# Moving the branches of an expert's second token block in a sparse expert loop

## The chip, the cores and the metric

One core of a Trainium2 chip runs the whole program as one launch. The metric is device time in microseconds (us): the median of 3 executions is 1828.38 us (1827.23 to 1830.39). Every trace number comes from one further execution that was profiled; it took 1832.22 us, of which the trace's span covers 1830.4 us.

Engines: PE is TensorE (PEld its weight loads), DVE is VectorE, ACT is ScalarE, POOL is GpSimd, and SP issues the large DMAs. Each works through its own instructions in the order in which they were written, and semaphores let one engine wait for another.

## The reference, cut to what matters

The program is one layer over 1024 tokens of 1024 channels: a token mixer and then a mixture of 32 experts, of which each token uses two. The change lies in the experts alone. The reference computes them so:

```python
def _expert_block(args):
    xblk, e = args                       # 128 token rows of one expert
    hid = jax.nn.silu(xblk @ w_gate[e]) * (xblk @ w_up[e])
    return hid @ w_down[e]
# block_e: an expert with n assigned tokens has ceil(n / 128) blocks
yb = lax.map(_expert_block, (xb, block_e))
out = jnp.einsum('tkd,tk->td', y.astype(f32), weights)
```

Gate and up weights are 1024 x 512, the down weight is 512 x 1024, all fp32. How many blocks an expert has is known only when the program runs.

## The kernel before, in words

The experts run one after another in a Python loop that is unrolled (`for e in range(NE)`, L1862). Each fp32 matrix is split into a high part (`hi`, a copy by ACT with rounding, L92) and a low part (`lo`, raw minus hi, by DVE, L93), and a product is summed from hi·hi, hi·lo and lo·hi (`mm3`, L96 to L98). An expert's weights are six loads of 1 MB (numbers 0 to 3 are gate and up, 4 and 5 down). `spl(e, i)` splits load `i` of expert `e` in two halves: two copies by ACT and two subtractions by DVE, and then SP issues a further load into the buffer that came free. The split halves go into ten buffers that are used in turn, so a new split waits until TensorE has done with what lay in its buffer.

For each expert the loop does:

- `xhalf` (L1686): four transposes of half of the 128 gathered tokens by PE into a `tp` buffer (there are two), then a split of the result by ACT and DVE. `XA` is the first half of the channels, `XB` the second.
- `part(e, q, os, ...)`: gate (`o` 0) and up (`o` 1) products over one half of the channels into two PSUM banks. An expert with at most 64 tokens takes a form with two products where others have three (L1697).
- `copies` (L1710): ACT copies the two sums out of PSUM (`sg`, `su`); DVE makes a small matrix `sm` (L1707).
- `fold` (L1719 to L1721): PE transposes both copies against `sm` into the two `tp` buffers, ACT takes silu, DVE multiplies, and the result is split into `hh` and `hl`.
- `down` (L96 to L98, `y<-...`): the down product, 24 matmuls, into the `y` banks.
- `emit`: DVE weighs the two banks into `yt` (L1736), POOL scatters them to memory (L1743).

While expert `e` is finished, the gate and up products of `e+1` are already begun: `part(e+1, 0, ...)` stands on both sides of `fold`. The two pairs of gate and up banks, `A` and `B`, change roles from expert to expert.

An expert with more than 128 tokens has a second block. It is done in `tc.If` blocks on a count that each engine loads into a register: `over(e, q, banks)` is transposes, split and products of the second block, `cso` are its copies (`og`, `ou`), and a fold, a down product and an `emit` of its own follow. The engines don't meet at such a block. An engine that skips it still adds, at its end, what the block's instructions would have added to its semaphore (an event at the line of the `If`). So an instruction behind the block that shares a tile with it waits until the other engine's sequencer has passed the block. With the inputs of this run 5 of the 32 experts have a second block (10 `yt` operations out of a `tp` buffer, two each).

In the kernel before, four such blocks stand in a round: L1871 (second half of `over` and `cso`), L1882 (the gather of a later second block), L1887 (fold of the second block) and L1893 (its down product at L1894, and at L1899 the first half of `over` of the next expert).

Of the kernel before, what the change touches and what calls it, by code (L numbers as in the profile page):

```python
# [20 lines left out]
P = 128  # L21
# [29 lines left out]
def block_kernel(ctx: ExitStack, tc: tile.TileContext, I, out):  # L51
# [3 lines left out]
    def pool(stack, name, bufs=1, **kw):  # L55
        return stack.enter_context(tc.tile_pool(name=name, bufs=bufs, reuse_waits="tile", **kw))
# [8 lines left out]
    def sb(pl, name, shape, dtype=F32, **kw):  # L65
        return pl.tile(shape, dtype, tag=kw.pop("tag", name), name=name, **kw)
# [24 lines left out]
    def split(hi, lo, src, eng=None):  # L91
        S.activation(hi, src, AF.Copy)  # L92
        (eng or V).tensor_tensor(lo, src, hi.bitcast(F32), op=ALU.subtract)  # L93

    def mm3(ps, a, b, first, last):
        PE.matmul(ps, a[0], b[0], start=first, stop=False)  # L96
        PE.matmul(ps, a[0], b[1], start=False, stop=False)  # L97
        PE.matmul(ps, a[1], b[0], start=False, stop=last)  # L98

    def warm(ps, us):  # L100
        for _ in range(round(us / 0.425)):
            PE.matmul(ps[:, 0:256], ident, ident.unsqueeze(1).to_broadcast([P, 2, P]), start=True, stop=True)
# [1079 lines left out]
    def granule(x, dtype=F32R):  # L1182
        a, b = (hip if x < NK - 3 else hia, lop) if x < NK else (hi2, lo2)
        return sb(a, "hi", [P, D], dtype), sb(b, "lo", [P, D], dtype)
# [337 lines left out]
    def dma_w():  # L1522
        x = next(ahead, None)
        if x is not None:
            RAW[x] = sb(bigp, "raw", [P, 2 * D])
            ld(RAW[x], I["w_exp"][seq[x[0]], x[1]])
        elif len(XL) < 5:
            t_ = sb(bigp, "raw", [P, 2, D])
            if len(XL) < 4:
                ld(t_, x1_d[2 * len(XL):2 * len(XL) + 2].rearrange("t p d -> p t d"))  # L1530
            else:
                ld(t_[:, 0], I["ln2_g"].partition_broadcast(P))
                ld(t_[:, 1], I["ln2_b"].partition_broadcast(P))
            XL.append(t_)
# [15 lines left out]
    def gather(xg, e, b):  # L1550
        if e < NE:
            G.indirect_dma_start(out=xg, out_offset=None, in_=h2_d,  # L1552
                                 in_offset=bass.IndirectOffsetOnAxis(ap=tbi[:, b, seq[e], 0:1], axis=0),
                                 bounds_check=T - 1, oob_is_err=False)
# [99 lines left out]
    psm = pool(mo, "psm", space=PSUM)  # L1654
# [6 lines left out]
    def spl(e, i, parts=(0, 1), refill=True):  # L1661
        if e >= NE:
            return
        for n in parts:
            a, b = granule(next(gi) % (NK + 2))
            split(a, b, RAW[e, i][:, n * D:(n + 1) * D], G if (i, n) in POOL_LO else V)
            SP[e, i, n] = (a, b)
        if 1 in parts:
            del RAW[e, i]
            if refill:  # L1670
                dma_w()

    def piece(e, i, k, n):
        z, w = n * k // D, n * k % D
        return tuple(t_[:, w:w + n] for t_ in SP[e, i, z])
# [6 lines left out]
    def xhalf(xg, q, nm="x"):  # L1682
        xs = sb(wk, f"{nm}{q if nm == 'x' else 0}", [P, 4, P, 2], F32R)
        pt = sb(psm, "tp", [P, 4, P], bufs=2)
        for z in range(4):
            PE.transpose(pt[:, z, :], xg[:, (4 * q + z) * P:(4 * q + z + 1) * P], ident)  # L1686
        split(xs[:, :, :, 0], xs[:, :, :, 1], pt)
        return xs
# [16 lines left out]
    def copies(e, pgu, nm="s", blk=0):  # L1705
        fm = sb(wk, nm + "m", [P, P])
        V.scalar_tensor_tensor(fm, both, few[:, blk, seq[e]:seq[e] + 1], ident, op0=ALU.mult, op1=ALU.add)  # L1707
        cs = [sb(wk, nm + x, [P, FF]) for x in "gu"]
        for c, ps_ in zip(cs, pgu):
            S.activation(c, ps_, AF.Copy)  # L1710
        return cs, fm

    def fold(cs, a="hh", b="hl"):
        (g, u), fm = cs
        a, b = sb(wk, a, [P, 4, P], F32R), sb(wk, b, [P, 4, P], F32R)
        pts = [sb(psm, "tp", [P, 4, P], bufs=2) for _ in range(2)]
        for src, pt in ((g, pts[0]), (u, pts[1])):
            for k in range(4):
                PE.matmul(pt[:, k, :], src[:, k * P:(k + 1) * P], fm, start=True, stop=True)  # L1719
        S.activation(g, pts[0].rearrange("p a b -> p (a b)"), AF.Silu)  # L1720
        V.tensor_mul(g, g, pts[1].rearrange("p a b -> p (a b)"))  # L1721
        split(a, b, g.rearrange("p (a b) -> p a b", a=4))
        return a, b

    def down(e, hs, py):
        for k in range(4):
            w = piece(e, 4 + k // 2, k % 2, D)
            for n in range(2):
                c = slice(n * 512, (n + 1) * 512)
                mm3(py[n], (hs[0][:, k, :], hs[1][:, k, :]), (w[0][:, c], w[1][:, c]), k == 0, k == 3)  # L1730

    def weigh(py, e, b):
        yt = sb(wk, "yt", [P, D])
        for n in range(2):
            c = slice(n * 512, (n + 1) * 512)
            V.scalar_tensor_tensor(yt[:, c], py[n], tbf[:, b, seq[e], 2:3], g2[:, c], op0=ALU.mult, op1=ALU.mult)  # L1736
        return yt

    def emit(py, e, b):
        scatter(weigh(py, e, b), e, b)  # L1740

    def scatter(yt, e, b):
        G.indirect_dma_start(out=y_d, out_offset=bass.IndirectOffsetOnAxis(ap=tbi[:, b, seq[e], 1:2], axis=0),  # L1743
                             in_=yt, in_offset=None, bounds_check=2 * T - 1, oob_is_err=False)

    def over(e, q, banks):
        if q == 0:
            warm(banks[0], 1.3)
        xs = xhalf(xos[e % 2], q, "o")
        part(e, q, range(2), xs, banks, 1)  # L1750
# [37 lines left out]
    def get_nb(e):  # L1788
        if e not in NBV:
            NBV[e] = load_nb(e)  # L1790
        return NBV[e]
# [14 lines left out]
    ybank = [sb(psm, f"y{n}", [P, 512]) for n in range(2)]  # L1806
# [55 lines left out]
    for e in range(NE):  # L1862
        nxt = e + 1 < NE
        A, B = GU[e % 2], GU[(e + 1) % 2]
        if nxt:
            XA = xhalf(xgs[(e + 1) % NX], 0)
            few_nb(e + 1)
        part(e, 1, range(2), XB, A)
        cs = copies(e, A)
        spl(e + 1, 1)  # L1870
        with tc.If(get_nb(e) > 1):  # L1871
            over(e, 1, B)
            cso = copies(e, B, "o", 1)
        if not nxt:
            spl(e, 4)
            spl(e, 5)
        if nxt:
            spl(e, 4)
            part(e + 1, 0, (0,), XA, B)
        hs = fold(cs)  # L1880
        if e + 2 < NE:
            with tc.If(get_nb(e + 2) > 1):  # L1882
                gather(xos[e % 2], e + 2, 1)
        if nxt:
            spl(e, 5)
            part(e + 1, 0, (1,), XA, B)
        with tc.If(get_nb(e) > 1):  # L1887
            h_ = fold(cso, "oh", "ol")
        if nxt:
            XB = xhalf(xgs[(e + 1) % NX], 1)  # L1890
            gather(xgs[(e + 1) % NX], e + 1 + NX, 0)
            down(e, hs, ybank)
        with tc.If((load_pair(e) if nxt else get_nb(e)) > 1):  # L1893
            with tc.If(get_nb(e) > 1):  # L1894
                banks = [sb(psm, "tp", [P, 512], bufs=2) for _ in range(2)]
                down(e, h_, banks)
                emit(banks, e, 1)
            if nxt:
                with tc.If(get_nb(e + 1) > 1):  # L1899
                    over(e + 1, 0, A)  # L1900
        if not nxt:
            down(e, hs, ybank)
            wf = sum([list(granule(next(gi) % (NK + 2), F32)) for _ in range(6)], [])
            with tc.If(load_nb(nbm) > 2):
                overflow(wf)
            for _ in range(3):
                y_raw()
            YT += [wf[2 * i:2 * i + 2] for i in range(5)]
            for i in range(NT):
                y_load(i)  # L1910
            tk = sb(wk, "tk", [P, NT])
            V.scalar_tensor_tensor(tk, iota[:, 0:NT], -float(P), tbf[:, 0, seq[e], 0:1].to_broadcast([P, NT]), op0=ALU.mult, op1=ALU.add)
            oh = xgs[2]
            for i in range(NT):
                V.tensor_scalar(oh[:, i * P:(i + 1) * P], iota[:, 0:P], tk[:, i:i + 1], None, op0=ALU.is_equal)
        spl(e + 1, 2)
        spl(e + 1, 3)
        if nxt:
            emit(ybank, e, 0)
        spl(e + 2, 0)  # L1920
# [9 lines left out]
    banks = [GU[0], GU[1], [sb(psm, "tp", [P, 512], bufs=2) for _ in range(2)], ybank]  # L1930
# [125 lines left out]
```

## Time and profile before

| | |
|---|---|
| median of 3 runs | 1828.38 us |
| the profiled execution | 1832.22 us, span 1830.4 us |
| PE busy | 1593.2 us, 87% of the span |
| DVE busy | 1338.5 us, 73% |
| ACT busy | 769.1 us, 42% |
| POOL busy | 308.4 us, 17% |
| loop over the experts | from about 905 us to 1755 us in the span |

An engine's busy share is an average over stages. The loop's stretch has to be read by itself: which engine waits in it, for whom, and what ends the wait. In the rows below "ACTq L1871" names an engine's sequencer at a line: the wait ended when ACT had passed the block at L1871.

### The profile page before, as it was taken

To read this page: it belongs to the slowest core of one execution; us is meant where nothing else is said; L and a number is where in the kernel's file an instruction comes from. 1 tells how busy PE (TensorE), PEld (TensorE's weight loads), DVE (VectorE), ACT (ScalarE), POOL (GpSimd) and SP (SyncE) were. 2 spreads that over 40 slices of the span, in tenths; PEclk is the share of its full clock that TensorE was granted. 3 is DMA by queue.
4 is the path that set the end of the run, shared out by engine and by line. 5 is a ranking of instruction groups with operands and counts; after the bars stand their busy time and mean duration, and the time that the engine had idled before them with its cause. 6 is when DMAs were issued, how large, how long until landed. Compare 5 with 4: busy or idle time off the path is not lost. (4 is left out here: it accounts for less than half of the span.)

```text
span 1830.4 us, 24156 instructions
## 1 busy us (share of the span) xinstructions
PE 1593.2 (87%) x7662; PEld 1256.8 (69%) x7662; DVE 1338.5 (73%) x2961; ACT 769.1 (42%) x1126; POOL 308.4 (17%) x264
## 2 busy tenths in 40 slices
PE   7999999999988999998877878777787888879775
PEld 3788887788877877887666656666566666767652
DVE  7768854699975787877757567777657777475768
ACT  2433323421133422212156455666556666464532
POOL 1530000022242000221211011011111111020117
PEclk9999999999999999998999998999999899999987
DMA  8327788523257564643448567788748778575663
GB/s 319 134 72 231 213 255 266 190 98 101 74 138 173 179 197 154 242 184 119 146 152 300 198 241 271 288 287 302 265 152 317 260 291 299 186 266 184 230 253 122
DMA packets 141759, 382.05 MB, mean 209 GB/s; under 512 B 17632, under 2 KB 76160, under 8 KB 116992
## 3 DMA queue, kind: packets, MB, share of 16 engines
q1 hardware_dynamic: 130912, 362.80, 57.4%
q0 software_dynamic: 10656, 16.80, 2.5%
q8 instruction: 108, 1.77, 0.4%
q14 instruction: 83, 0.68, 0.1%
HBM read 336.98 MB, written 68.76 MB: 222 GB/s over the span
## 5 line engine op out<-in xcount | busy, mean ns | idle before, releaser
L93 DVE TENSOR_TENSOR lo<-raw,hi 128x1024 fp32r<-128x1024 f32 x376 | 442.8, 1221 | 147.2 <-ACT hi L92 138.8
L92 ACT ACTIVATE hi<-raw 128x1024 fp32r<-128x1024 f32 x376 | 373.4, 1049 | 119.3 <-PEq L1893 39.8
L96 PE MATMUL g<-hh,wh 128*128 128x512 f32 x448 | 176.9, 395 | 0.0
L98 PE MATMUL g<-hh,wl 128*128 128x512 f32 x448 | 174.7, 390 | 0.0
L97 PE MATMUL g<-hl,wh 128*128 128x512 f32 x448 | 174.6, 390 | 0.0
L1743 POOL DMA_INDIRECT y_d<-yt,tbi x37 | 65.9, 1780 | 399.0 <-DVE yt L1736 300.3
L1697 PE MATMUL g<-hi,x 128*128 128x512 f32 x168 | 76.9, 458 | 54.4 <-DVE x L93 37.7
L96 PE MATMUL y<-hi,hh 128*128 128x512 f32 x256 | 108.1, 422 | 5.1 <-ACTq L1887 5.1
L1552 POOL DMA_INDIRECT xg<-h_d,tbi x32 | 40.4, 1264 | 381.8 <-PE tp L1686 314.7
L98 PE MATMUL y<-hi,hl 128*128 128x512 f32 x256 | 104.6, 409 | 0.0
L97 PE MATMUL y<-lo,hh 128*128 128x512 f32 x256 | 104.3, 407 | 0.0
L96 PEld LDWEIGHTS g<-hh,wh 128*128 128x128 f32 x448 | 84.1, 188 | 19.1 <-issue 2.3
L98 PEld LDWEIGHTS g<-hh,wl 128*128 128x128 f32 x448 | 84.1, 188 | 18.0
L93 POOL TENSOR_TENSOR wl<-raw,wh 128x1024 fp32r<-128x1024 f32 x17 | 41.0, 2409 | 329.4 <-ACT wh L92 329.4
L97 PEld LDWEIGHTS g<-hl,wh 128*128 128x128 f32 x448 | 84.1, 188 | 16.7
L1686 PE MATMUL tp<-ident,xg 128*128 128x128 f32 x256 | 41.3, 285 | 54.5 <-ACTq L1887 40.1
L1697 PEld LDWEIGHTS g<-hi,x 128*128 128x128 f32 x168 | 35.0, 208 | 71.8 <-ACTq L1871 60.9
L1686 PEld LDWEIGHTS tp<-ident,xg 128*128 128x128 f32 x256 | 27.4, 141 | 77.8 <-ACTq L1887 51.2
L611 ACT ACTIVATE sg<-g 128x512 f32<-128x512 f32 x32 | 19.2, 599 | 140.1 <-PE g L98 104.8
L1697 PE MATMUL g<-lo,x 128*128 128x512 f32 x168 | 74.1, 441 | 1.6 <-DVE lo L93 1.6
L912 DVE TENSOR_TENSOR vs<-vs,sa 128x32 f32<-128x32 f32 x512 | 75.2, 201 | 0.0
L1697 PE MATMUL u<-hi,x 128*128 128x512 f32 x168 | 67.7, 403 | 0.0
(537 smaller groups left out, 3868.3 us busy)
## 6 DMA issues: line engine op xcount, KB each, us to landing
raw<-in_w_exp SPq DMA_DIRECT2D x192, 1024.0 KB
raw<-in_w_r SPq DMA_DIRECT2D x28, 512.0 KB
w<-w_d SPq DMA_DIRECT2D x32, 384.0 KB
raw<-in_w_ada SPq DMA_DIRECT2D x20, 512.0 KB
sig_d<-sg SPq DMA_DIRECT2D x32, 256.0 KB
rp<-r_d SPq DMA_DIRECT2D x64, 128.0 KB
raw<-in_w_ada SPq DMA_DIRECT2D x6, 1024.0 KB
aw<-in_w_ada SPq DMA_DIRECT2D x12, 512.0 KB
```

What stands on the lines that cost most here:

```text
L92: S.activation(hi, src, AF.Copy)
L93: (eng or V).tensor_tensor(lo, src, hi.bitcast(F32), op=ALU.subtract)
L96: PE.matmul(ps, a[0], b[0], start=first, stop=False)
L97: PE.matmul(ps, a[0], b[1], start=False, stop=False)
L98: PE.matmul(ps, a[1], b[0], start=False, stop=last)
L611: S.activation(sg, pg, AF.Sigmoid)
L912: V.tensor_tensor(new[:, d], new[:, d], t[d][:, r], op=ALU.add)
L1552: G.indirect_dma_start(out=xg, out_offset=None, in_=h2_d, in_offset=bass.IndirectOffsetOnAxis(ap=tbi[:, b, seq[e], 0:1], axis=0), bounds_c ...
L1686: PE.transpose(pt[:, z, :], xg[:, (4 * q + z) * P:(4 * q + z + 1) * P], ident)
L1697: PE.matmul(banks[o], xs[:, z, 0:HB].rearrange("p t x -> p (t x)"), w[x], start=(q == 0 and z == 0 and x == 0), stop=(q == 1 and z == 3 an ...
L1743: G.indirect_dma_start(out=y_d, out_offset=bass.IndirectOffsetOnAxis(ap=tbi[:, b, seq[e], 1:2], axis=0), in_=yt, in_offset=None, bounds_ch ...
```

## The change

The order of the instructions in a round is altered; none is added or taken away except that blocks are cut differently. The copies `sg` and `su` (with `sm`) now stand behind the split of load 1 and behind the block of `over(e, 1, ...)`. The split of load 5 is done in two halves, one on each side of the last gate and up products and `XB`. `XB` stands right behind those products, ahead of the block that held the second block's fold. That block is joined with the first half of the next expert's `over` and stands ahead of the main down product; the second block's own down product and `emit` stand in a block of their own behind it.

```diff
         part(e, 1, range(2), XB, A)
-        cs = copies(e, A)
         spl(e + 1, 1)
         with tc.If(get_nb(e) > 1):
             over(e, 1, B)
             cso = copies(e, B, "o", 1)
-        if not nxt:
-            spl(e, 4)
-            spl(e, 5)
+        cs = copies(e, A)
+        spl(e, 4)
         if nxt:
-            spl(e, 4)
             part(e + 1, 0, (0,), XA, B)
         hs = fold(cs)
         if e + 2 < NE:
             with tc.If(get_nb(e + 2) > 1):
                 gather(xos[e % 2], e + 2, 1)
+        spl(e, 5, (0,))
         if nxt:
-            spl(e, 5)
             part(e + 1, 0, (1,), XA, B)
-        with tc.If(get_nb(e) > 1):
-            h_ = fold(cso, "oh", "ol")
-        if nxt:
             XB = xhalf(xgs[(e + 1) % NX], 1)
             gather(xgs[(e + 1) % NX], e + 1 + NX, 0)
-            down(e, hs, ybank)
+        spl(e, 5, (1,))
         with tc.If((load_pair(e) if nxt else get_nb(e)) > 1):
             with tc.If(get_nb(e) > 1):
-                banks = [sb(psm, "tp", [P, 512], bufs=2) for _ in range(2)]
-                down(e, h_, banks)
-                emit(banks, e, 1)
+                h_ = fold(cso, "oh", "ol")
             if nxt:
                 with tc.If(get_nb(e + 1) > 1):
                     over(e + 1, 0, A)
+        if nxt:
+            down(e, hs, ybank)
+        with tc.If(get_nb(e) > 1):
+            banks = [sb(psm, "tp", [P, 512], bufs=2) for _ in range(2)]
+            down(e, h_, banks)
+            emit(banks, e, 1)
```

ACT's instructions from the first half of the next tokens to the silu, in a round of the kernel before (`x` is that half, `hi<-raw` are weight copies, `o`, `og` and `ou` belong to the second block):

```order
L92 ACTIVATE x_11531<-tp 128x512
L1710 ACTIVATE sg<-g_9282 128x512
L1710 ACTIVATE su<-u_9283 128x512
L92 ACTIVATE hi<-raw 128x1024 x2
L1871 COMPARE_AND_BRANCH
L92 ACTIVATE o_11600<-tp 128x512
L1692 UNCONDITIONAL_BRANCH
L1710 ACTIVATE og<-g_9280 128x512
L1710 ACTIVATE ou<-u_9281 128x512
L1871 UNCONDITIONAL_BRANCH x2
L1692 UNCONDITIONAL_BRANCH
L92 ACTIVATE hi<-raw 128x1024 x2
```

The same round on ACT after the change:

```order
L92 ACTIVATE x_11531<-tp 128x512
L92 ACTIVATE hi<-raw 128x1024 x2
L1870 COMPARE_AND_BRANCH
L92 ACTIVATE o_11594<-tp 128x512
L1692 UNCONDITIONAL_BRANCH
L1710 ACTIVATE og<-g_9280 128x512
L1710 ACTIVATE ou<-u_9281 128x512
L1870 UNCONDITIONAL_BRANCH x2
L1692 UNCONDITIONAL_BRANCH
L1710 ACTIVATE sg<-g_9282 128x512
L1710 ACTIVATE su<-u_9283 128x512
L92 ACTIVATE hi<-raw 128x1024 x2
```

The two copies of the sums moved from ahead of two weight copies and the block (L1871, now L1870) to behind them.

PE's instructions from the last gate and up product of the next expert to the main down product before (`tp<-ident,xg` are the transposes of `XB`, `tp<-om,...` the second block's fold, `y` the down product):

```order
L98 MATMUL u_9281<-hi,x_12349 128x512
L1692 UNCONDITIONAL_BRANCH
L1887 COMPARE_AND_BRANCH
L1719 MATMUL tp<-om,og 128x128 x4
L1719 MATMUL tp<-om,ou 128x128 x4
L1887 UNCONDITIONAL_BRANCH x2
L1686 MATMUL tp<-ident,xg_9275 128x128 x4
L96 MATMUL y_9284<-hi,hh 128x512
L97 MATMUL y_9284<-lo,hh 128x512
```

The same place on PE after the change, as far as the next expert's second block begins:

```order
L98 MATMUL u_9281<-hi,x_12349 128x512
L1692 UNCONDITIONAL_BRANCH
L1686 MATMUL tp<-ident,xg_9275 128x128 x4
L1794 TENSOR_LOAD nbp
L1887 COMPARE_AND_BRANCH
L1888 COMPARE_AND_BRANCH
L1719 MATMUL tp<-om,og 128x128 x4
L1719 MATMUL tp<-om,ou 128x128 x4
L1888 UNCONDITIONAL_BRANCH x2
L1891 COMPARE_AND_BRANCH
L102 MATMUL g_9282<-ident 128x256 x3
```

And PE from the end of that block to the main down product, after the change:

```order
L98 MATMUL u_9283<-hi,o_12616 128x512
L1692 UNCONDITIONAL_BRANCH
L1891 UNCONDITIONAL_BRANCH
L1887 UNCONDITIONAL_BRANCH
L96 MATMUL y_9284<-hi,hh 128x512
L97 MATMUL y_9284<-lo,hh 128x512
L98 MATMUL y_9284<-hi,hl 128x512
```

The transposes of `XB` now come ahead of the block. The register load, the joined block and its end, which stood behind the down product (L1893), now stand between `XB` and the down product.

## Rows read from the trace of the kernel before

**Rows 1.** Busy time by stretch: PE, PEld, DVE, ACT, POOL; clock, DMA share, GB/s:
```profile
1230.62:1253.63 23.01, 18.43 (x89) 14.55 (x88) 18.33 (x19) 15.29 (x18) 3.05 (x2) 1.00 0.80 290
1088.37:1300.66 212.29, 167.59 (x752) 131.99 (x752) 163.96 (x171) 136.08 (x162) 27.94 (x19) 0.94 0.79 288
1018.68:1088.37 69.69, 56.71 (x254) 45.09 (x254) 42.94 (x47) 35.78 (x44) 7.94 (x5) 0.93 0.54 197
941.54:1750.60 809.06, 656.03 (x2945) 519.43 (x2943) 566.78 (x602) 467.95 (x564) 103.76 (x66) 0.94 0.70 254
```
**Rows 2.** PE's waits, 890 to 1750 us (total, times, longest):
```profile
PE tp L1686 <- ACTq L1887: 40.1, 26, 2.6
PE g L1697 <- DVE x L93: 37.7, 12, 3.3
PE g L96 <- ACTq L1871: 21.6, 8, 2.8
PE g L1697 <- ACTq L1871: 15.7, 6, 2.6
```
**Rows 3.** Timeline of PE in one period (start, us, ..., idle before <-releaser):
```profile
1240.11 0.51 PE L1697 MATMUL g<-hi,x 128*128 128x512 f32 x1 [2.62 <-ACTq L1871]
...
1247.46 0.66 PE L1686 MATMUL tp<-ident,xg 128*128 128x128 f32 x4 [1.60 <-ACTq L1887]
...
1253.93 0.30 PE L1686 MATMUL tp<-ident,xg 128*128 128x128 f32 x1 [0.30 <-PEq L1893]
```
**Rows 4.** Timeline of ACT in the same period:
```profile
1230.81 3.91 ACT L92 ACTIVATE hi<-raw 128x1024 fp32r<-128x1024 f32 x4 [2.89 <-issue]
...
1237.52 0.60 ACT L1710 ACTIVATE su<-u 128x512 f32<-128x512 f32 x1 [1.26 <-PE u L98]
1238.02 1.99 ACT L92 ACTIVATE hi<-raw 128x1024 fp32r<-128x1024 f32 x2
...
1253.81 3.90 ACT L92 ACTIVATE hi<-raw 128x1024 fp32r<-128x1024 f32 x4 [2.81 <-issue]
```
**Rows 5.** Timeline of DVE in the same period:
```profile
1231.90 2.36 DVE L93 TENSOR_TENSOR lo<-raw,hi 128x1024 fp32r<-128x1024 f32 x2 [2.54 <-ACT hi L92]
...
1239.10 2.36 DVE L93 TENSOR_TENSOR lo<-raw,hi 128x1024 fp32r<-128x1024 f32 x2 [0.39 <-ACT hi L92]
1241.67 2.36 DVE L93 TENSOR_TENSOR lo<-raw,hi 128x1024 fp32r<-128x1024 f32 x2 [0.21 <-DVEq L1871]
...
1245.50 0.69 DVE L93 TENSOR_TENSOR hl<-sg,hh 128x512 fp32r<-128x512 f32 x1 [0.70 <-ACT hh L92]
1246.45 2.36 DVE L93 TENSOR_TENSOR lo<-raw,hi 128x1024 fp32r<-128x1024 f32 x2 [0.26 <-ACT hi L92]
...
1250.09 2.36 DVE L93 TENSOR_TENSOR lo<-raw,hi 128x1024 fp32r<-128x1024 f32 x2 [0.44 <-ACT hi L92]
```
**Rows 6.** Splitting of weights, lines by cost, 890 to 1750 us:
```profile
L93 DVE TENSOR_TENSOR lo<-raw,hi 128x1024 fp32r<-128x1024 f32 x370 | 435.8, 1221 | 143.5 <-ACT hi L92 136.4 <-DVEq L1871 5.6 <-issue 1.6
L92 ACT ACTIVATE hi<-raw 128x1024 fp32r<-128x1024 f32 x370 | 367.5, 1049 | 116.4 <-issue 38.7 <-PEq L1893 37.0 <-PEq L1899 31.4
```
**Rows 7.** Timeline of PE's waits around one expert with a second block:
```profile
1022.58 0.47 PE L1697 MATMUL g<-hi,o 128*128 128x512 f32 x1 [1.59 <-DVE o L93]
...
1037.25 0.76 PE L1697 MATMUL g<-hi,o 128*128 128x512 f32 x1 [4.28 <-DVE o L93]
...
1050.33 0.66 PE L1686 MATMUL tp<-ident,xg 128*128 128x128 f32 x4 [0.43 <-ACT og L1720]
...
1072.14 0.76 PE L1697 MATMUL g<-hi,x 128*128 128x512 f32 x1 [3.32 <-DVE x L93]
...
1082.20 0.66 PE L1686 MATMUL tp<-ident,xg 128*128 128x128 f32 x4 [1.61 <-ACTq L1887]
```
**Rows 8.** The page's 40 slices of the span: bytes moved, GB/s:
```profile
GB/s 319 134 72 231 213 255 266 190 98 101 74 138 173 179 197 154 242 184 119 146 152 300 198 241 271 288 287 302 265 152 317 260 291 299 186 266 184 230 253 122
```

## The prediction, made before the result was known

> **What bounds the kernel now.** I read the busy time by stretch first, then PE's waits, then the timelines of PE, ACT and DVE in one round, and last the splitting lines by cost and the page's rate of DMA. A period here runs from the end of one main down product to the end of the next. From 941.54 to 1750.60 us there are 30 of them in 809.06 us [rows 1]. Five experts have a second block; four of these stretch two periods each and the first stretches one, which makes 9 long periods and leaves 21 ordinary ones. The stretch of nine ordinary periods in rows 1 gives 212.29 / 9 = 23.59 us each. In it PE is busy 167.59 / 9 = 18.6 us a period and DVE 163.96 / 9 = 18.2 us: neither is full. So a round is a chain in which PE, ACT and DVE wait for each other, and the reader is to look for where they do.
>
> PE waits at two places in a round [rows 2]: for ACT's passing of L1887 ahead of the transposes of `XB` (40.1 us, 26 times), and ahead of the first gate product of the next expert, either for ACT's passing of L1871 (21.6 + 15.7 us) or for the low half of `XA` from DVE (37.7 us). In the period that I work with, whose clock is 1.00 throughout [rows 1], they are 1.60 and 2.62 us [rows 3].
>
> The cause of the 2.62 us is in ACT's row: `su` can be copied only when the product is done, two weight copies (1.99 us) come behind it, and only then comes the block L1871 [rows 4]. PE needs ACT past that block, since the block's copies read the bank that PE writes next.
>
> The third wait is DVE's: 2.54 us for `hi` [rows 5]. ACT starts those copies 0.19 us after the down product's end (1230.62), and again 0.18 us after the next one's (1253.63), after 2.89 and 2.81 us of idling [rows 4]. Over the loop `hi` waits 37.0 us for PE's passing of L1893 and 31.4 us of L1899, and the "issue" part, 38.7 us, has the same place in the round [rows 6]. I read it as one cause: their buffers held the next expert's load 0, which the block at L1899 could still read, and PE passes that block only behind the down product.
>
> **The change part by part, in an ordinary period.**
>
> *Copies behind the block.* ACT no longer has `su` and the two weight copies between it and the block. It is free of the late copies (below), so it reaches the block before the product's end: the copies of `x` (a small one, like `su`'s 0.6 us) and two of weights (2.0 us) against 6.9 us from the down product's end to the product's end (1240.11 - 2.62 - 1230.62). The 2.62 us become the plain end of a block, for which the nearest row is 0.30 us [rows 3]: 2.32 us saved on PE. What gets later is the fold's input: `sg` and `su` now stand right behind the product (two copies of 0.6 us) beside the eight or twelve matmuls of `part`, and `sm` stands behind two subtractions on DVE. Free if DVE is ahead; if not, up to 2.4 us of PE idling at the fold.
>
> *`XB` ahead of the block.* Its transposes need only that the silu has read the `tp` buffer, not ACT's copies of load 5. The 1.60 us go. What is late next is the low half of `XB`, which is needed only after the down product; transposes and product take 6.2 us (1247.46 to 1253.63).
>
> *The joined block ahead of the down product.* A register load, a compare and a block's end now stand on PE between `XB` and the down product. No row shows this place. Bounds: 0, if `hl` or load 5 is late anyway; 0.30 by the end of L1893, a block that is skipped likewise; 1.6 if it costs as much as L1887 did. I take 0.30. It would be less than nothing only if waiting there shortened another wait, which no row suggests.
> The block's end behind the down product stays (L1895 for L1893), at 0.30 as now.
> On the plus side the buffers of load 0 come free before the down product, so the four `hi` copies and the first two pairs of subtractions run beside it. DVE's 2.54 us go, and with the copies of the sums out of the way its 0.39 us too.
>
> [...]
>
> *Load 5 in halves.* Nothing is added; SP's load behind it is issued about one subtraction later. POOL's gather and scatter keep their places behind `XB` and `yt`. Cost nothing, since no split of weights waits for a load: DVE's 143.5 us are 136.4 for ACT, 5.6 and 1.6; of ACT's 116.4 us 107.1 are named, and none of it is a DMA [rows 6].
>
> *Sum for an ordinary period.* PE's side: 23.01 - 2.32 - 1.60 + 0.30 = 19.4 us. DVE's side: busy 18.33 [rows 1], and the idling that stays, 0.21 + 0.70 + 0.26 + 0.44 [rows 5], gives 19.9; the rows leave 0.14 of the 23.01 unnamed, so 20.1. DVE becomes the longer side, PE's remaining idling is waiting for the low half of `XA`. For the two sides not meeting exactly I add 0.1: 20.2 us against 23.59, which saves 3.4 us, times 21 = 71 us.
>
> *Long periods.* In a pair [rows 7] the 1.61 us go. The 4.28 us shrink: the second block's low half waits behind DVE's backlog, which is now some 3 us shorter. The 1.59 us grow by about 0.7, since `over` now comes before the down product, which had covered DVE's backlog. The 3.32 us stay: DVE's chain from the second `yt` to `x` is as it was. 1.6 + 2.9 - 0.7, plus the 0.43 us that go as the 1.61 do, less 0.2 for ends of blocks, is 4 us a pair: 16 us for four, and 4 for the first expert and its period: 20 us.
>
> Together 91 us: 1832.22 - 91 = 1741 us for the profiled execution, which ran 3.8 us above the median of the three runs. Against that median, 1828.4 - 91 = **1737 us**.
>
> Its own range: with PE's side alone deciding (19.4) and 8 us a pair, 4.2 x 21 + 36 = 124 us; with 21.3 us a period and half the gain in the pairs, 48 + 10 = 58 us. I trust neither end: 1712 to 1765.
>
> **The rivals.**
>
> *DMA becomes the bound.* A period moves 288 GB/s x 23.59 us = 6.8 MB [rows 1]. At 319 GB/s, the fastest slice of the span [rows 8], that takes 21.3 us, so 2.3 x 21 = 48 us and 20 in the long ones: 1760. For it: at 20.2 us the DMA share would be 0.92. Against: 0.79 of the engines carry the 288 today, and no split waits for a load. 0.12.
>
> *DVE's wait stays.* If the "issue" waits of `hi` are not the block's, DVE keeps its 2.54 us and the period falls only to 23.01 - 0.39 = 22.6: 1.0 x 21 = 21 us at most, 1807. PE's two stalls would then reappear as one on the low half of `XA`, as it does 12 times already. For it: 38.7 us carry no name. Against: the start 0.2 us behind the down product's end, twice. 0.08.
>
> *Slower: PE resumes late behind the joined block.* Place: between `XB` and the down product, every round. Price: its stall, beyond what PE can spare. PE's side has 0.7 us in hand (20.1 - 19.4) and the gain is 3.4 us a period plus 20 / 21 from the long ones, so it decides from 0.7 + 3.4 + 1.0 = 5.1 us a period up; at 6 us the kernel takes about 0.9 x 21 = 19 us more, 1847. For it: a new point where PE must come to rest with nothing queued behind. Against: 0.30 us at the like place. 0.05. [...]
>
> *It does not do what it says:* the transposes and the first product still wait for a point of ACT behind the work that was moved, and the stalls change names at one size. 0.05, 1828.
>
> **How the numbers follow.** The forecast has 0.70. Less than 0.2% (3.7 us) either way can't be told from no change. Faster: 0.70 + 0.12 + 0.08 = 0.90; same 0.05; slower 0.05. The range of 1712 to 1790 holds about 0.65 of the 0.70, the whole DMA case and a part of the case in which DVE's wait is only half gone.
>
> **What would show it.** Right: no PE waits for ACT's sequencer at the first gate product or at `XB` beyond 0.5 us a round; ACT's `hi` copies running during the down product; DVE busy above 85% in ordinary stretches, PE's remaining waits named DVE `x`; periods of about 20 us. Wrong: `hi` still starting at the down product's end; waits for a DMA of `raw`; a gap of more than 1 us ahead of the first `y` matmul; long waits of the fold for `sm`.

## The result and the profile after

The kernel after takes 1747.77 us (median of 4 runs, 1745.63 to 1749.76), the kernel before 1829.39 us (4 runs, 1827.23 to 1830.4). The ratio is 0.9555 [0.9539, 0.9572]: 81.6 us faster, where 91 were forecast. The profiled execution took 1748.59 us, its span 1746.8 us, and the mean granted clock of TensorE rose from 0.953 to 0.972.

From the ends of the main down products in the two traces:

| stretch | before, us | after, us | difference | forecast |
|---|---|---|---|---|
| start to the end of the first expert's down product | 941.5 | 942.3 | +0.8 | -2 |
| first expert's long period | 30.8 | 29.0 | -1.8 | -2 |
| 17 ordinary periods, by themselves | 404.1 | 342.1 | -62.0 | -58 |
| four groups of one ordinary and two long periods | 374.1 | 350.9 | -23.2 | -30 |
| last round | 20.2 | 17.2 | -3.1 | none |
| behind the last down product | 59.6 | 65.3 | +5.7 | none |
| span | 1830.4 | 1746.8 | -83.6 | -91 |

(The forecast put 4 us on the first expert and its period together; they stand here half and half.)

Busy time by stretch: nine ordinary periods in a row, one of them, a group of one ordinary and two long ones, and all 30 (columns as in [rows 1]; these windows lie 0.4 us behind the ends of the down products, which changes no length).

```profile
1080.44:1261.41 180.97, 162.02 (x753) 126.56 (x753) 162.67 (x172) 134.22 (x163) 43.60 (x19) 0.97 0.91 335
1201.17:1220.61 19.44, 18.45 (x89) 14.60 (x90) 17.82 (x20) 14.96 (x19) 4.87 (x2) 1.00 0.93 344
1020.49:1080.44 59.95, 50.67 (x229) 39.58 (x230) 36.89 (x42) 31.42 (x40) 9.35 (x5) 0.94 0.53 188
942.71:1664.77 722.06, 637.23 (x2944) 498.53 (x2942) 565.33 (x603) 461.82 (x564) 137.88 (x66) 0.97 0.77 283
```

180.97 / 9 = 20.1 us a period, where [rows 1] has 23.6. DVE's busy time hardly changes (163 for 164 us) and PE's falls by 6 us for the same number of matmuls (162 for 168, beside a mean granted clock of 0.97 for 0.94), so most of the 31 us that went is idling: DVE is now busy for 162.67 / 180.97 = 90% and PE for 162.02 / 180.97 = 90%. DMA carries 335 GB/s where it carried 288.

Four of PE's waits from 890 to 1680 us, then three of the stretch of nine periods alone:

```profile
PE g L1697 <- DVE x L93: 31.3, 14, 3.5
PE tp L1719 <- DVE x L93: 8.4, 5, 2.4
PE g L98 <- DVE x L93: 7.2, 9, 1.7
PE g L1697 <- DVE o L93: 4.7, 3, 1.6
```
```profile
PE g L1697 <- DVE x L93: 9.3, 5, 1.9
PE tp L1719 <- DVE sm L1707: 1.9, 4, 0.7
PE y L96 <- PEq L1887: 0.3, 1, 0.3
```

The 40.1 us for ACT's passing of the block ahead of `XB` and the 37.3 us for the copies' block [rows 2] are gone. What is left is mostly DVE's `x`, the low half of `XA`, as forecast; the 8.4 us at the fold are new and belong to the second blocks (see `XB` alone below).

PE in the period 1201.17 to 1220.61, against [rows 3]:

```profile
1201.06 0.63 PE L1686 MATMUL tp<-ident,xg 128*128 128x128 f32 x4 [0.30 <-PEq L1895]
...
1208.11 0.47 PE L1697 MATMUL g<-hi,x 128*128 128x512 f32 x1 [0.48 <-PEq L1870]
...
1213.71 0.60 PE L1686 MATMUL tp<-ident,xg 128*128 128x128 f32 x4
1214.46 0.47 PE L96 MATMUL y<-hi,hh 128*128 128x512 f32 x1
```

The 2.62 us have become 0.48, the block's own end. The 1.60 us ahead of `XB` are gone, and past the joined block PE loses 1214.46 - 1213.71 - 0.60 = 0.15 us.

Ordinary periods are not of one kind. Three of them, by the ends of their own down products (columns as above):

```profile
1121.08:1140.50 19.42, 18.47 (x88) 14.60 (x88) 17.80 (x19) 14.93 (x19) 4.87 (x2) 1.00 0.91 342
1220.21:1240.57 20.36, 18.00 (x80) 14.14 (x80) 18.04 (x20) 14.83 (x19) 4.88 (x2) 0.92 0.95 341
1348.20:1367.89 19.69, 16.64 (x80) 12.92 (x80) 17.78 (x20) 14.66 (x18) 3.88 (x2) 1.00 0.89 331
```

In the first, and in three more of the 17 that stand by themselves (19.42 to 19.44 us), PE is busy for 95% and doesn't wait for DVE: there PE sets the length. In the other 13 (19.7 to 20.9 us) PE waits 0.5 to 1.9 us for DVE's `x`.

ACT and DVE in the period 1201.17 to 1220.61, against [rows 4, 5]:

```profile
1207.67 0.60 ACT L1710 ACTIVATE su<-u 128x512 f32<-128x512 f32 x1 [1.27 <-PE u L98]
1208.16 2.00 ACT L92 ACTIVATE hi<-raw 128x1024 fp32r<-128x1024 f32 x2
...
1216.18 5.80 ACT L92 ACTIVATE hi<-raw 128x1024 fp32r<-128x1024 f32 x6 [0.27 <-ACTq L1887]
```
```profile
1206.40 0.69 DVE L93 TENSOR_TENSOR x<-tp,x 128x512 fp32r<-128x512 f32 x1
...
1213.51 0.69 DVE L93 TENSOR_TENSOR hl<-sg,hh 128x512 fp32r<-128x512 f32 x1 [0.70 <-ACT hh L92]
1214.46 1.23 DVE L93 TENSOR_TENSOR lo<-raw,hi 128x1024 fp32r<-128x1024 f32 x1 [0.25 <-ACT hi L92]
...
1217.94 4.63 DVE L93 TENSOR_TENSOR lo<-raw,hi 128x1024 fp32r<-128x1024 f32 x4 [0.52 <-DVEq L1895]
```

The down product starts at 1214.46, and 1.7 us later ACT begins six weight copies beside it, which ran behind it before. DVE's 2.54 us for `hi` are gone. The splitting lines over the whole span show the same:

```profile
L93 DVE TENSOR_TENSOR lo<-raw,hi 128x1024 fp32r<-128x1024 f32 x376 | 443.3, 1220 | 63.9 <-ACT hi L92 50.1
L92 ACT ACTIVATE hi<-raw 128x1024 fp32r<-128x1024 f32 x376 | 373.1, 1048 | 14.3 <-ACTq L1887 6.0
```

143.5 us of idling ahead of DVE's subtractions [rows 6] have become 63.9, and the 116.4 us ahead of ACT's copies 14.3, the unnamed part of them included.

Behind the last down product, PE and then DVE, after:

```profile
1689.80 2.04 PE L1934 MATMUL g<-yt,xg 128*128 128x512 f32 x2 [8.26 <-DVE yt L1736]
```
```profile
1674.84 2.36 DVE L93 TENSOR_TENSOR lo<-raw,hi 128x1024 fp32r<-128x1024 f32 x2 [0.26 <-ACT hi L92]
1684.50 1.53 DVE L1910 SCALAR_TENSOR_TENSOR tk<-iota,tbf 128x8 f32<-128x8 f32 x1 [7.30 <-DVEq L1902]
```

And DVE at the same place of the kernel before:

```profile
1762.97 0.69 DVE L93 TENSOR_TENSOR hl<-sg,hh 128x512 fp32r<-128x512 f32 x1 [0.70 <-ACTq L1887]
1770.68 0.17 DVE L1912 SCALAR_TENSOR_TENSOR tk<-iota,tbf 128x8 f32<-128x8 f32 x1 [7.02 <-DVEq L1904]
```

DVE needs some 7 us to get past the skipped block of the last expert, before and after. What is new are the two subtractions ahead of it (2.36 us, load 5 of the last expert, whose split the diff cut in two). They make DVE come to the block later: it is past it at 1684.50, 3.0 us behind the last down product's end (1681.5), where before it was past at 1770.68, just ahead of that end (1830.4 - 59.6 = 1770.8). PE sees that wait now: 8.26 us ahead of its next product, for `yt`.

### The profile page after: what moved, and what is told of

Read it like the earlier page. It is cut to its first block, busy times and chain, and to the rows that moved or that the text cites. A ratio compares the mean times of both kernels' runs of the same rounds, so it can differ in the third digit from the quotient of the medians.

```text
span 1746.8 us, 24156 instructions
## 1 busy us (share of the span) xinstructions
PE 1575.4 (90%) x7662; PEld 1234.9 (71%) x7662; DVE 1336.9 (77%) x2961; ACT 763.0 (44%) x1126; POOL 342.5 (20%) x264
## 5 line engine op out<-in xcount | busy, mean ns | idle before, releaser
L93 DVE TENSOR_TENSOR lo<-raw,hi 128x1024 fp32r<-128x1024 f32 x376 | 443.3, 1220 | 63.9 <-ACT hi L92 50.1
L92 ACT ACTIVATE hi<-raw 128x1024 fp32r<-128x1024 f32 x376 | 373.1, 1048 | 14.3 <-ACTq L1887 6.0
L96 PE MATMUL g<-hh,wh 128*128 128x512 f32 x448 | 177.6, 397 | 0.0
L1743 POOL DMA_INDIRECT y_d<-yt,tbi x37 | 90.1, 2434 | 369.6 <-DVE yt L1736 351.8
L96 PE MATMUL y<-hi,hh 128*128 128x512 f32 x256 | 104.5, 408 | 8.6 <-ACT hh L92 3.0
L1697 PE MATMUL g<-hi,x 128*128 128x512 f32 x168 | 74.8, 445 | 33.6 <-DVE x L93 31.3
L1552 POOL DMA_INDIRECT xg<-h_d,tbi x32 | 46.4, 1449 | 287.1 <-PEq L1887 143.7
L96 PEld LDWEIGHTS g<-hh,wh 128*128 128x128 f32 x448 | 84.6, 189 | 19.1 <-issue 2.3
L1697 PE MATMUL g<-lo,x 128*128 128x512 f32 x168 | 73.2, 436 | 2.1 <-DVE lo L93 2.1
L1697 PEld LDWEIGHTS g<-hi,x 128*128 128x128 f32 x168 | 34.0, 203 | 50.3 <-ACT hi L92 38.8
L92 ACT ACTIVATE x<-tp 128x512 fp32r<-128x512 f32 x64 | 40.0, 627 | 67.6 <-PE tp L1686 67.6
L1697 PE MATMUL u<-hi,x 128*128 128x512 f32 x168 | 67.7, 403 | 0.0
L1697 PE MATMUL u<-lo,x 128*128 128x512 f32 x168 | 66.7, 397 | 0.0
```

Of the source, the lines that this page charges most:

```text
L1552: G.indirect_dma_start(out=xg, out_offset=None, in_=h2_d, in_offset=bass.IndirectOffsetOnAxis(ap=tbi[:, b, seq[e], 0:1], axis=0), bounds_c ...
L1697: PE.matmul(banks[o], xs[:, z, 0:HB].rearrange("p t x -> p (t x)"), w[x], start=(q == 0 and z == 0 and x == 0), stop=(q == 1 and z == 3 an ...
```

## The experiments

Two theories were to be told apart. *Chain*: a round is closed by two sides, PE's (with its two waits) and DVE's (with its wait for `hi`), and a wait that goes counts only as far as the other side lets it. *Additive*: each of the three moves has its own worth. The first kernels make one move alone in the kernel before.

**Copies alone**

```diff
-        cs = copies(e, A)
         spl(e + 1, 1)
         with tc.If(get_nb(e) > 1):
             over(e, 1, B)
             cso = copies(e, B, "o", 1)
+        cs = copies(e, A)
```

> The kernel before with one part of the change: the copies of the sums behind the split of load 1 and the block L1871. Chain theory (a round has a PE side and a DVE side, and a wait that goes counts only as far as the other side lets): PE's 2.62 us turn into a wait for the low half of XA, which DVE finishes 7.8 us after the down product as before; the period falls by DVE's 0.39 us only, some 10 us in all, 1819 us. Additive theory (each wait of PE that goes is worth its size): 2.32 us x 21, 1780 us.

Measured: 1801.53 us, 0.9834 [0.9803, 0.9865], ordinary periods of 22.78 us. Its waits, PE and DVE (890 to 1750 us):

```profile
PE g L1697 <- DVE x L93: 45.1, 18, 3.3
PE g L96 <- ACTq L1870: 13.9, 8, 1.8
PE tp L1686 <- ACTq L1887: 34.6, 26, 1.9
DVE lo L93 <- ACT hi L92: 117.3, 94, 9.1
```

In the rounds whose first product is at L1697 PE no longer waits for ACT there but for DVE's `x` (37.7 us before [rows 2]); in the eight at L96 it still waits for ACT's passing of the block, 13.9 us for 21.6. DVE still waits for `hi`. The stall got smaller and in part changed its name. Both theories missed the total; the chain's level of 22.6 us was near, but the kernel before starts from a mean of 23.77 over the 17 ordinary periods that stand by themselves, not from the 23.0 of the one period that was read, whose clock was 1.00.

**`XB` alone**

```diff
-        with tc.If(get_nb(e) > 1):
-            h_ = fold(cso, "oh", "ol")
         if nxt:
             XB = xhalf(xgs[(e + 1) % NX], 1)
             gather(xgs[(e + 1) % NX], e + 1 + NX, 0)
+        with tc.If(get_nb(e) > 1):
+            h_ = fold(cso, "oh", "ol")
+        if nxt:
             down(e, hs, ybank)
```

> The kernel before with one part of the change: XB's transposes and the gather ahead of the block with the second block's fold. Both theories: PE's 1.60 us ahead of XB go, the down product ends earlier by it, and the hi copies that wait for its end start earlier by it, so DVE's side gets shorter too: 1.5 x 21 plus some 6 us in the long periods, about 1791 us. If the wait moves to hl or load 5 ahead of the down product instead: 1829 us.

Measured: 1815.27 us, 0.9919 [0.9896, 0.9943]. The total is 16 us, not the 38 of the sum: the expectation missed. Ordinary periods fell by 1.41 us, as expected; the four groups with long periods did not fall (377.2 for 374.1 us). A wait of PE ahead of the second block's fold, which the kernel before doesn't have, shows why:

```profile
PE tp L1719 <- DVE x L93: 11.3, 5, 3.4
```

In the four groups the waits for ACT at L1887 (10.4 us) went, but 7.9 us of this new wait came, and PE's busy time grew from 310.5 to 316.3 us for the same matmuls at a lower clock (0.91 to 0.95, for 0.94 to 0.96). `XB` uses one of the two `tp` buffers, and now it stands ahead of that fold, which needs both: the fold waits until DVE has split `XB`. The runs bear this out: the wait stands in every kernel here that has `XB` ahead of that fold, and is missing before, with the copies alone, with the joined `over` alone and without `XB` ahead.

**Joined block's `over` alone**

```diff
-            down(e, hs, ybank)
-        with tc.If((load_pair(e) if nxt else get_nb(e)) > 1):
-            with tc.If(get_nb(e) > 1):
-                ...
-            if nxt:
+            with tc.If(load_pair(e) > 1):
                 with tc.If(get_nb(e + 1) > 1):
                     over(e + 1, 0, A)
+            down(e, hs, ybank)
+        with tc.If(get_nb(e) > 1):
+            ...
```

> The kernel before with one part of the change: the first half of the next expert's second block stands ahead of the main down product, so PE gives load 0's buffers back before it. Chain theory: DVE's 2.54 us ahead of lo go, but PE still waits for ACT at L1871 and L1887, which come from ACT's order; PE's side stays at 23 us: 1825 us, within 5 us of before. DVE-alone theory (DVE's idling is all that sets the period): 2.5 x 21, about 1776 us.

Measured: 1841.79 us, 1.005 [1.0027, 1.0074], so a little slower. PE's waits (890 to 1770 us, the whole loop):

```profile
PE g L1697 <- ACTq L1871: 39.3, 15, 2.6
PE tp L1686 <- ACTq L1887: 34.4, 26, 1.7
PE g L96 <- ACTq L1871: 21.0, 8, 2.6
```

PE's two stalls stand, ordinary periods are as they were (23.75 us), and the early start of DVE's work buys nothing. The groups with long periods got 13 us longer (386.9 for 374.1), and PE's busy time in them grew as much for the same matmuls (322.9 for 310.5 us), beside a lower clock (0.91 to 0.95, for 0.94 to 0.96). That DVE alone sets the round (1776) is refuted.

**All but the copies** (the kernel after, with `cs = copies(e, A)` back ahead of `spl(e + 1, 1)`)

> The changed kernel with the copies of the sums put back ahead of the split of load 1. Chain theory: PE keeps the wait at the first gate product, su plus two weight copies plus the block, about 2.6 us; the period is PE's, 23.0 - 1.6 + 0.3 = 21.7 us against 20.1 with the copies moved: 1.6 x 21 = 34 us above the changed kernel, 1782 us. Additive theory: the copies' 2.32 us x 21 = 49 us above, 1797 us.

Measured: 1792.15 us, 0.978 [0.9739, 0.9821], 44 us above the kernel after, between the chain's 1782 and the additive 1797; ordinary periods 21.51 us (the chain: 21.7). What goes beyond the chain's sum lies outside them: the groups with long periods take 374.5 us, as before the change, where the kernel after takes 350.9.

```profile
PE g L1697 <- ACTq L1871: 39.3, 15, 2.6
PE g L96 <- ACTq L1871: 21.0, 8, 2.6
```

The copies' stall is back at 2.6 us, and it alone takes 44 us here, while its going alone was worth 29.

**Without the join ahead** (copies and `XB` moved; `over(e + 1, 0, A)` and the second block's down product stay in their block behind the main down product; load 5 is split whole, as before the change)

> Two parts of the change: copies behind the block and XB ahead of it; the first half of the next expert's second block stays behind the main down product. Chain theory: load 0's buffers come free at the down product's end, DVE's four subtractions and yt stand ahead of XA's low half, 7.8 us after it, so sm, fold and hl are late: about 21.0 us a period, 0.9 x 21 = 19 us above the changed kernel, 1767. Additive theory: this part alone gave nothing (0.02 us a period), so nothing is lost: 1748.

Measured: 1787.53 us, 0.9771 [0.9737, 0.9804]; ordinary periods 21.65 us. One wait each of PE, DVE and ACT (890 to 1705 us, the whole loop):

```profile
PE g L1697 <- DVE x L93: 45.6, 18, 3.3
DVE lo L93 <- ACT hi L92: 69.7, 72, 7.5
ACT hi L92 <- PEq L1894: 31.6, 17, 2.6
```

With the block behind the down product ACT again waits for PE's passing of it, DVE for ACT, and PE for DVE's `x`: the chain in three rows. It costs 40 us, more than the chain had put on it (19).

**Without `XB` ahead** (copies and joined `over` moved; `XB` stays behind the second block's fold, which keeps a block of its own; load 5 is split whole)

> Two parts of the change: copies behind the block, and the next expert's second block ahead of the main down product; XB stays behind the block with the fold of the second block. Chain theory: PE keeps a wait for ACT's copies of load 5 ahead of XB, and DVE's side (20.1) hides a part of it: about 20.8 us a period, 0.7 x 21 = 14 us above the changed kernel, 1762. Additive theory: what XB gave alone, 1.4 x 21 = 30 us above: 1778.

Measured: 1755.7 us, 0.959 [0.9559, 0.962]; ordinary periods 20.54 us. Two of PE's waits (890 to 1680 us):

```profile
PE tp L1686 <- ACTq L1887: 35.5, 26, 2.0
PE g L1697 <- DVE x L93: 16.4, 10, 3.4
```

The stall ahead of `XB` is back almost whole (35.5 for 40.1 us [rows 2]), yet the kernel loses only 8 us: in most periods DVE's side is the longer one, and PE's wait for `x` shrank from 31.3 to 16.4 us in exchange. The four periods that PE had set got 2.2 us longer (21.66 for 19.43 us in the mean); the other 13 did not get longer in the mean.

Together:

| move | alone | taken out of the whole change |
|---|---|---|
| copies behind the block | -29 | +44 |
| `XB` ahead | -16 | +8 |
| joined block ahead of the down product | +11 | +40 |
| sum | -34 | +92 |

All three at once bring 82 us. The additive theory falls. The moves two by two say where they meet: copies and `XB` without the join bring 43 us, about the sum of the two (45); copies with the join bring 75, where the sum is 18; `XB` with the join brings 39, where the sum is 5. The two lower rows of the last column hold one thing more: those kernels split load 5 whole, which by itself saves some 2 to 3 us at the end of the loop (see the last expert below). Load 5 in halves was not run alone in the loop.

**More work for DVE** (the kernel after, one subtraction of 128x1024 done twice, 1.13 us a round)

```diff
             split(a, b, RAW[e, i][:, n * D:(n + 1) * D], G if (i, n) in POOL_LO else V)
+            if (i, n) == (3, 1):
+                V.tensor_tensor(b, RAW[e, i][:, n * D:(n + 1) * D], a.bitcast(F32), op=ALU.subtract)
```

> The changed kernel with one subtraction of 128x1024 done twice by DVE in every round (1.13 us from start to start). If DVE's side sets the ordinary period: 1.1 x 21 = 23 us more and little in the long periods, where DVE idles: 1771 us. If PE or the loads set it: under 5 us more, 1752.

Measured: 1790.51 us, 0.9781 [0.9756, 0.9806]; ordinary periods 21.86 us. PE's longest wait in total, and the same three periods as shown for the kernel after:

```profile
PE g L1699 <- DVE x L93: 47.3, 18, 3.3
```
```profile
1130.48:1151.15 20.67, 18.64 (x88) 14.57 (x88) 19.01 (x20) 14.95 (x19) 3.74 (x2) 1.00 0.90 324
1239.51:1261.14 21.63, 18.01 (x80) 14.16 (x80) 19.29 (x21) 14.86 (x19) 3.73 (x2) 0.92 0.89 322
1374.04:1396.96 22.92, 19.29 (x81) 15.44 (x80) 19.02 (x21) 14.69 (x18) 2.75 (x2) 0.85 0.82 285
```

DVE's side is the longer one, or level with PE's: a period grew by 1.73 us, more than the work put in, and PE waits for `x`. The periods show where the surplus lies. In ten of the 17 the mean granted clock is the same as in the kernel after, and they grew by 0.9 to 1.3 us, 1.2 in the mean, about the work put in; the second row above is one (20.36 before the extra work). In the other seven the clock is lower, and they grew by 1.9 to 3.2 us; the third row is one (19.69 at a clock of 1.00). The first is one of the four that PE had set (19.42), so there the two sides were nearly level.

**More work for PE** (the kernel after, five matmuls of 128x512 ahead of each main down product, their result overwritten by it; 1.14 us a round, 35 us in all)

```diff
+            for _ in range(5):
+                PE.matmul(ybank[0], hs[0][:, 0, :], piece(e, 4, 0, D)[0][:, 0:512], start=True, stop=True)
             down(e, hs, ybank)
```

> The changed kernel with five more matmuls ahead of every main down product (into a bank that the product then overwrites; 5 x 0.23 = 1.14 us). If DVE's side sets the ordinary period, PE has about 1.0 us in hand there (2.1 us idle a period less 1.1 at the ends of blocks), and pays in full in the 9 long ones: 0.4 x 21 + 10 = 18 us more, 1766. If PE sets it: 1.14 x 31 = 35 us, 1783. If the loads set it: under 10 us.

Measured: 1755.62 us, 0.9594 [0.9573, 0.9616]. The mean of the ordinary periods is the same (20.15 for 20.13 us), but three things cancel in it. The first two of the three periods shown for the kernel after:

```profile
1117.80:1138.30 20.50, 19.55 (x93) 15.59 (x93) 17.87 (x19) 15.05 (x19) 4.88 (x2) 1.00 0.87 319
1219.18:1238.86 19.68, 17.78 (x85) 13.84 (x85) 18.05 (x20) 15.09 (x19) 4.87 (x2) 1.00 0.98 361
```

The four periods that PE set pay the added work in full (19.43 to 20.57 us in the mean). Seven are the same within 0.1 us: there PE had this much in hand, and DVE's side sets the length. Six got 0.7 us shorter, and in these the mean granted clock rose from 0.92 to 1.00. In the profiled executions the long periods grew by 13 us (10 were expected), and the parts ahead of the loop and behind it were 7 us shorter.

**The last expert's load 5 split early** (for the last expert both halves ahead of the fold)

```diff
         spl(e, 4)
+        if not nxt:
+            spl(e, 5)
...
-        spl(e, 5, (0,))
+        if nxt:
+            spl(e, 5, (0,))
...
-        spl(e, 5, (1,))
+        if nxt:
+            spl(e, 5, (1,))
```

> The changed kernel, but for the last expert alone both halves of load 5 are split ahead of the fold, as before the change. The stretch behind the last down product was 5.3 us longer than before; DVE reached the skipped block at L1902, which takes 6 us to pass in both kernels, only after two subtractions that now stand behind the fold. If that is the cause: about 2.6 us less, 1745. If the 5.3 us are the slower clock there or the scatter: no change.

Measured: 1744.23 us, 0.953 [0.951, 0.955], 3.5 us less in the median, with intervals that overlap; the stretches show it more plainly. The last round takes 20.2 us again and the stretch behind it 58.6, where the kernel after has 17.2 and 65.3: together 3.7 us less. DVE comes past the skipped block here:

```profile
1677.69 0.17 DVE L1914 SCALAR_TENSOR_TENSOR tk<-iota,tbf 128x8 f32<-128x8 f32 x1 [6.40 <-DVEq L1906]
```

That is 1.3 us ahead of the last down product's end (1679.0), where the kernel after was 3.0 behind it. So the net loss at the end of the loop comes from those two subtractions standing behind the fold, ahead of the skipped block; 3 of the 5.7 us in the table only moved there from the last round.

**A part of DVE's subtractions by POOL** (the kernel after with `POOL_LO = ((3, 1),)`: one in twelve)

> The changed kernel with one of the twelve weight subtractions of a round (load 3, second half) given to POOL, 2.4 us there. If DVE's side sets the ordinary period: it falls towards PE's 19.4 us, 0.6 x 21 = 13 us less, 1735. If the loads are the bound (share 0.91 of the DMA engines now): no change, 1748. If POOL's gather and scatter get late behind it, or DVE slows beside it: more than 1750.

Measured: 1752.1 us, 0.958 [0.9561, 0.9598], so 4 us worse; ordinary periods 20.17 us (20.13). The lines of DVE and POOL, 900 to 1700 us, and DVE's shortest, median and longest subtraction (ns):

```profile
L93 DVE TENSOR_TENSOR lo<-raw,hi 128x1024 fp32r<-128x1024 f32 x345 | 447.8, 1334 | 63.6 <-ACT hi L92 50.8 <-DVEq L1895 11.0 <-ACTq L1887 1.0
L93 POOL TENSOR_TENSOR lo<-raw,hi 128x1024 fp32r<-128x1024 f32 x31 | 89.1, 2873 | 135.0 <-ACT hi L92 56.9 <-PE y L98 41.8 <-DVE lo L93 19.1
```
```profile
L93 DVE TENSOR_TENSOR lo<-raw,hi x345: 1206/1218/3432, 903.4 to 1682.2; 128x1024 fp32r<-128x1024 f32 x173
```

DVE does 31 fewer, but its busy time is not less (447.8 for 443.3 us). Most subtractions take what they took (the median is 1218 ns); 26 of the 345 take 2.1 to 3.4 us, and each of these overlaps one by POOL. That is the third case of the expectation.

**The weighing of `y` by ACT** (on top of the early split of load 5)

```diff
     def emit(py, e, b):
-        scatter(weigh(py, e, b), e, b)
+        yt = sb(wk, "yt", [P, D])
+        for n in range(2):
+            S.activation(yt[:, n * 512:(n + 1) * 512], py[n], AF.Copy, scale=tbf[:, b, seq[e], 2:3])
+        scatter(yt, e, b)
...
+        spl(e + 2, 0)
         if nxt:
             emit(ybank, e, 0)
-        spl(e + 2, 0)
...
+            V.tensor_mul(YT[i][0], YT[i][0], g2)
```

> The changed kernel with the last expert's load 5 split ahead of the fold, and with yt written by ACT (a copy scaled by the token's weight) behind the split of the next load 0, not by DVE; the factor per channel is multiplied in once per 128 tokens at the end, 8 more DVE multiplications of 1.2 us there. If DVE sets the round: its 1.33 us go, PE's 19.4 us or the loads come next; 0.9 x 21 + 1.3 x 9 = 30 us less in the loop, 3 less at its end as in the run with that split alone, up to 10 more in the last stretch: 1722 us. If the loads are the bound (share 0.91): no more than the 3 us, 1745 to 1755.

Measured: 1730.16 us (1728.45 to 1732.7), 0.9453 [0.9426, 0.9479]: faster than both kernels. Ordinary periods fell to 18.8 us. Eight multiplications by `g2` moved to the end, and the stretch behind the last down product grew from 58.6 to 75.9 us, 17 us where up to 10 were expected. One stretch of the loop (columns as in [rows 1]):

```profile
1080.44:1261.41 180.97, 167.00 (x800) 131.39 (x799) 160.28 (x162) 153.51 (x191) 29.43 (x20) 1.00 0.93 355
```

With two DVE operations less a round, DMA carries 355 GB/s: the 335 of the kernel after was no ceiling. PE is now the busiest engine (167.00 / 180.97 = 92%). The ordinary periods that PE had set stay as they were (19.45 for 19.43 us); the others fell, to between 17.4 and 19.7.

## Why the prediction was right, step by step

- *Ordinary periods*: 20.13 us for a forecast of 20.2. The 17 by themselves gave 62.0 us; the four in the groups, from 90.6 us to 4 x 20.1, about 10 more: 72 where 71 were forecast. The mechanism holds for most of them: PE waits for DVE's `x` in 13 of the 17, 1.13 us more work on DVE cost 43 us and 1.14 on PE 8. But that the mean is met so closely is partly luck. The very period from which the two sides were worked out (23.01 us) takes 19.44 now, which is PE's side of the sum (19.4), not DVE's (20.1). And the forecast set a period at a clock of 1.00 against a mean of 23.59 us at 0.94: 0.6 of its 3.4 us is the step from that mean to the period read, for which the sum has no term. The clock did rise, to 0.97, and PE's busy time in the 30 periods fell from 656.03 [rows 1] to 637.23 us for the same matmuls.
- *Copies*: 2.62 us became 0.48, for 0.30 put down. The fold does wait for `sm` now and then (1.9 us in nine periods), far within the 2.4 us a period that were allowed.
- *`XB`*: gone as said. Taken out of the whole change it costs only 8 us, since PE has slack in most periods; the sum by sides, not by stalls, had this in it.
- *Joined block*: 0.15 us past it in the period shown, for 0.30 put down. The rival in which PE resumes late there falls: PE's waits for its own passing of the joined block (L1887, L1891) ahead of the down product come to 2.1 us in all 30 periods, the longest 0.5, and no run shows there the 6 us at which that rival was priced.
- *`hi` beside the down product*: as said. The kernel without the join shows ACT's wait for PE's passing of the block by name, and with the join the unnamed "issue" waits went along with the named ones (116.4 us became 14.3), so they were rightly read, and the rival in which DVE's wait stays falls.
- *Long periods*: the step with a wrong size. 16 us were forecast for the four pairs, some 13 came. The 4.28 us wait for the second block's low half went down to 1.58 us, as a backlog that shrinks would have it. The 1.59 us, which were to grow by 0.7, did not (1.55 at that place, now named as DVE's passing of L1895). The 3.32 us stayed, as forecast (3.31). The 1.61 us went. But new waits of up to 2.4 us, which the sum doesn't have, stand at the second block's fold (PE `tp` for DVE `x`, 8.4 us in five): `XB` ahead of it holds a `tp` buffer that it needs.
- *Last rounds*: not in the sum. The last round gained 3.1 us and the stretch behind it lost 5.7. "Load 5 in halves costs nothing" failed there: the last expert has no next tokens whose products could hide the two late subtractions, and the skipped block behind it is slow to pass (DVE idles there for 7.30 us).
- *Start*: the stretch up to the first expert's down product was 0.8 us longer, not 2 shorter. But the part ahead of the expert loop, which the change leaves alone, ended between 881 and 888 us in all kernels here: at 885.6 before (the table ahead of the prediction has about 905) and 887.9 after. From there to that down product's end it is 55.9 us before and 54.4 after, so 1.5 of the 2 us came.
- *DMA as the bound*: fell. 335 GB/s at a share of 0.91, and 355 at 0.93 in the last experiment, against the 319 on which that rival was priced.

The forecast for the single moves was poorer than for the whole: copies alone were to give some 10 us and gave 29, the kernel without the join was to lose 19 and lost 40. What a single stall is worth is read less well from one undisturbed period than from all of them, which differ by up to 4 us.

## What to carry to other kernels

Where engines skip a data-dependent block one by one, the block is a point of order for whoever shares a tile with it (before, PE waited 40.1 us in all for ACT's passing of one such block [rows 2]): put ahead of it nothing that it doesn't need, and behind it what others don't wait for. Work out both sides of such a round and take the longer one; moves on different sides are worth little alone and can even lose, but together they add what neither shows. Then look at the last iteration, where the work that covers a moved step is missing. And read the rounds one by one: a mean that stays can hide rounds that got longer and others that got shorter.

## What was not expected of the hardware

- *A skipped block can be slow to pass.* DVE idles for 7.30 us at L1902 (7.02 at L1904 before), a block which it skips: 6.2 us lie between its branch and the event at the block's end. ACT takes 4.7 us there. PE passes the joined block in 0.15 us. The instruction queues in the ten microseconds around it, after (1676 to 1686 us), move more than in the loop:

```profile
q8 instruction: 2, 0.03, 1.3%
q14 instruction: 3, 0.02, 0.6%
```

These are 5 packets. From 942 to 1660 us the two queues move 103, 1.4 in ten microseconds and never more than 4. But no run here is without these packets, so what makes this block slow is not shown.
- *DVE's and POOL's subtractions were slower beside each other.* POOL's 31 took 2.87 us in the mean, where 17 of that size on POOL ahead of the loop took 2.42 in the kernel after. 26 of DVE's 345 took 2.1 to 3.4 us, each overlapping one by POOL, while DVE's median stayed at 1.22. What holds them up is not shown.
- *The mean granted clock differed between the kernels*: 0.953 before, 0.972 after, 0.977 when PE was given more work, 0.959 when DVE was. How much of the 82 us the clock brought was not separated.
